# Row sums of two norms from two wide matmuls with ones as weights, in a single-core decoder block

## The chip, the core and the metric

The kernel runs on one core of a Trainium2 chip. Its time is device microseconds from start to end of one execution; the median over the runs is what counts. All matrix products are exact to nearly float32: each float32 operand is split into a high part and a low part (both of type `F32R`, which TensorE takes in one pass), and a product is the sum high*high + high*low + low*high, accumulated in float32.

## The reference

One block of a hybrid decoder over 512 positions and 1024 channels:

```python
def rmsnorm(x, g):
    y = x * lax.rsqrt(jnp.mean(x * x, axis=-1, keepdims=True) + EPS)
    return y * g

h = rmsnorm(x, norm1_g)                # norm 1
proj = h @ w_in                        # short conv, attention q/k/v, gates
...                                    # sparse attention, gated short conv
x = x + mix @ w_o
h = rmsnorm(x, norm2_g)                # norm 2
gu = h @ w_ffn_in                      # 1024 -> 2 x 2816
g = causal_dwconv(gu[..., :D_FF], ffn_conv_w) + ffn_conv_b
x = x + (silu(g) * gu[..., D_FF:]) @ w_ffn_out
```

Both norms need, for each of the 512 tokens, the sum of 1024 squares, and from it the factor r = (sum/1024 + eps)^-0.5.

## The kernel before

Channels lie on the 128 partitions (8 tiles of 128 channels), tokens along the free dimension (512). The norm's factor depends on the token alone, so the kernel multiplies by the gains at once, runs its products on the unscaled x, and applies r to the results. For r it squares each tile (ScalarE), adds the eight tiles up elementwise (`sq_sum` in norm 1, `sq2` in norm 2, 128x512 each), and then has to add over the 128 partitions. That is the work of `row_scales`. Before the change it goes like this, for four groups of 128 tokens:

1. Four float32 matmuls (L417): a 128x128 block of the summed squares is the weights, two columns of ones move through, and the result has the tokens on the partitions, two equal columns for each group, in a PSUM bank `pr`.
2. VectorE (L420) scales these 128x4 sums and adds eps into `ms`.
3. GpSimd (L411) raises `ms` to the power -0.5: `r`, 128x4, tokens on partitions.
4. Four transposes on TensorE (L426) of `r`, broadcast along the free dimension, bring r to all partitions with the tokens along the free dimension; ScalarE (L428) copies that from PSUM into `rb`.

**Norm 1** stands in the first stage, the token projection. `tok_round` walks over eight weight chunks k = 0..7; for token tiles 0 and 1 it runs 350-wide products into the banks `pj_s` (tile 0) and `pj_t`/`pj_o` (tile 1), `tok_products` being one chunk of one tile: products with the high weights at L219 and L220, with the low ones (`tok_lo`) at L222. At k = 6, `between` finishes an extra product `pkc` (compressed keys and values), has ScalarE copy it out of PSUM (`kv_evac`, `kc`, L471), and calls `row_scales`. VectorE and ScalarE then scale `pj_*` by r as they read the banks (`qkv`, L608 and L610). **Norm 2** stands between the output projection, whose loop ends with x in `x1` and its high and low forms `xf_h`, `xf_l`, and the feed-forward stage.

**The feed-forward stage** goes over 22 tiles of 128 inner channels, in pairs f = 0, 2, 4, ... For each pair there is a gate half (n = 0) and an up half (n = 1), and each half is a 2x2 block product made by seven products instead of eight (`ff_pair`; a11, a12, a22 and sums of them, named 1, 2, 3 and 4, are the forms of the weights, banks `p1`, `p26`, `p37`, `p45` take the results). Weights come in as two 512 KB loads for each half on SyncE's queue (`wr_s0_4` is half 0 of pair 4: in the order's names `wr_s0_40` and `wr_s0_41` are its two loads), through three buffers `wr` that the down-projection's loads `wr_d` share. A load is issued when the last reader of an older buffer is done.

The forms are made on ScalarE (`wh_s`, `sh`, `th`: high parts) and VectorE (`s32`, `s41`: sums of blocks at L945 to L950, `sl`, `tl`: low parts at L902). For some loads the low part is not made on VectorE: ScalarE writes the negated high part (`lo_by_dma`, L924, into `wl_s` or `wl_d`) and GpSimd starts a second, adding load of the same weights onto it (L927). The results are combined on VectorE (`c` for the gate, `up` for the up half, L1092 and L1120), multiplied by `rb_n2` (L1128, L1132), convolved (`cv`, L1074 to L1076) and passed through silu (L1077, ahead of whose first use ScalarE loads a function table), split (`ah`, `al`) and used by the down-projection (`pdn`).

The order of instructions on each engine is not written out by hand: the program is traced in a source order and a scheduler (`schedule_with_timeline_sim=True`, L1259) chooses each engine's order by a timeline of its own. `behind(later, earlier)` adds an order between two instructions. So an edit in one place can move instructions far from it.

Of the kernel before, what the change touches and what calls it, by code (L numbers as in the profile page):

```python
# [11 lines left out]
F32 = mybir.dt.float32  # L12
# [6 lines left out]
P = 128  # L19
D = 1024  # L20
# [71 lines left out]
def tile_block(ctx: ExitStack, tc: tile.TileContext, xT, pos, par, par2, w_tok, w_a3, w_gate, w_ao, w_bo, w_o,  # L92
# [93 lines left out]
        return hi, lo  # L186


    ones = const([P, P], "ones")
    nc.gpsimd.memset(ones, 1.0)  # L190
    warm = const([P, 1], "warm")
    wu = d_bank("wu")
# [19 lines left out]

    tok_lo = [y_tile(f"tok_lo{i}") for i in range(4)]

    def tok_products(tt, bank, k, wh, wl, first, last):
        ts_ = slice(tt * P, (tt + 1) * P)
        for c, (a, b) in enumerate(CH):
            acc = bank[c][:, :b - a]
            nc.tensor.matmul(acc, xg_h[:, k, ts_], wh[c], start=first, stop=False)  # L219
            nc.tensor.matmul(acc, xg_l[:, k, ts_], wh[c], start=False, stop=False)  # L220
        for c, (a, b) in enumerate(CH):
            nc.tensor.matmul(bank[c][:, :b - a], xg_h[:, k, ts_], wl[:, a:b], start=False, stop=last)  # L222
# [20 lines left out]
    def tok_round(tts, on_k, between):  # L243

        banks = [tok_banks(tt) for tt in tts]
        for k in range(KD):
            h = th.tile([P, TOKC], F32R, name=f"th{k}", tag="th", bufs=LAG) if k < LAG else None
            wh, wl = on_k(k, lambda first=0, then=None: load_w(w_tok[k], TOKC, f"t{tts[0]}{k}", first=first, mid=k > 0,
                                                               lo=tok_lo_of(k), hi=h, then=then, pieces=k == 0,
                                                               cuts=[b for _, b in CH] if k < 2 else ()))  # L250
            if k < LAG:
                kept.append(h)
            if k == KD - 2:
                between(k)
            if k < 2:
                first_products(tts, banks, k, [wh[:, a:b] for a, b in CH], wl)
            for tt, bank in zip(tts, banks) if k > 1 else ():
                tok_products(tt, bank, k, [wh[:, a:b] for a, b in CH], wl, k == 0, k == KD - 1)
            if k < KD - 2:
                between(k)  # L260
        return banks
# [148 lines left out]

        nc.gpsimd.tensor_tensor(dst, src, mhalf[:, :n], op=ALU.pow)  # L411

    def row_scales(total, name, bank_of):

        pr = bank_of(f"pr_{name}")
        for t in range(NT):
            sums = nc.tensor.matmul(pr[:, 2 * t:2 * t + 2], total[:, t * P:(t + 1) * P], ones[:, 0:2],  # L417
                                    start=True, stop=True)
        ms = sb.tile([P, NT], F32, name=f"ms_{name}", tag="ms")
        nc.vector.tensor_scalar(ms, pr[:, 0:2 * NT].rearrange("p (t two) -> p t two", two=2)[:, :, 0], 1.0 / D, EPS,  # L420
                                op0=ALU.mult, op1=ALU.add)
        r = sb.tile([P, NT], F32, name=f"r_{name}", tag=f"r_{name}")
        rsqrt(r, ms, NT)

        for t in range(NT):
            rows = nc.tensor.transpose(pr[:, t * P:(t + 1) * P], r[:, t:t + 1].to_broadcast([P, P]), ident)  # L426
        rb = sb.tile([P, S], F32, name=f"rb_{name}", tag="rb")
        nc.scalar.activation(rb, pr, AF.Copy)  # L428
        return r, rb, (sums, rows)

# [22 lines left out]
    def between(k):  # L455
        if k in kv_made:
            kv_made.pop(k)()
        if k == KD - 2:
            for kv in range(2):
                kc2.append(kv_evac(kv))  # L460
            scales1.extend(row_scales(sq_sum, "n1", d_bank))

    kv_made = {}
    kc2, scales1 = [], []
# [21 lines left out]
    for m, f in ((cm_add, NEG), (cm_one, 0.0)):  # L486
        nc.gpsimd.affine_select(out=m, in_=m, compare_op=ALU.is_ge, fill=f, base=-(CMPB - 1),
                                pattern=[[P, NT], [-STRIDE, NC]], channel_multiplier=1)
    r1, r1b, _ = scales1
    r1sq = const([P, S], "r1sq", F32, pb)  # L490
    nc.scalar.activation(r1sq, r1b, AF.Square)

# [560 lines left out]
        if n > 0:  # L1053
            nc.vector.tensor_add(sq2, sq2, sq)
    first_rest(0)
    _, r2b, (sums2, rows2) = row_scales(sq2, "n2", d_bank)
    mx_ctx.close()
    xv_ctx.close()

# [204 lines left out]
```

## Time and profile before

| | |
|---|---|
| Time, median of 3 runs | 724.91 us (724.86 to 725.02) |
| Profiled execution, its own time | 724.8 us |
| Its span on the core | 722.8 us (2.0 us lie around it) |
| TensorE (PE) busy | 717.5 us, 99% |
| Weight loads (PEld) busy | 638.6 us |
| VectorE (DVE) busy | 574.2 us, 79% |
| ScalarE (ACT) busy | 413.6 us, 57% |
| GpSimd (POOL) busy | 121.8 us, 17% |
| Granted TensorE clock | 1.00 throughout |

How to read it: rows of the timeline give start, duration, engine, line, operation, output<-inputs and the count of like instructions in the row, and in brackets the idle time of the engine ahead of it with what ended it. Matmuls are pipelined, so the duration of one is longer than its share of the engine: that share is the distance between two starts. An engine's share of busy time is a mean over stages with different limits.

### The profile page before, as it was taken

What the parts mean: (1) busy time and instruction counts of PE and PEld (TensorE: products, weight loads), DVE (VectorE), ACT (ScalarE), POOL (GpSimd) and SP (SyncE); (2) the same over time, 40 slices, a digit from 0 to 9 for tenths busy, and PEclk for the clock granted to TensorE, in tenths of its full rate; (3) what the DMA queues carried; (4) which work ended last, traced back from release to release, by engine and by line L of the source; (5) the groups of instructions that cost most, each with busy time, mean ns of one, the idle gap of its engine ahead of it and who ended that gap; (6) DMA issues with size and microseconds to landing.
All of it is one profiled execution on the core that took longest, in us unless ns stands there. A gap on an engine that the chain in (4) does not pass through costs nothing.

```text
span 722.8 us, 11204 instructions
## 1 busy us (share of the span) xinstructions
PE 717.5 (99%) x4281; PEld 638.6 (88%) x4281; DVE 574.2 (79%) x985; ACT 413.6 (57%) x705; POOL 121.8 (17%) x111
## 2 busy tenths in 40 slices
PE   9999999999999999999999999999999999999997
PEld 8999888888888888878889999999999999999986
DVE  7869967687666676787876999999898988979833
ACT  7666555777767676544665666565455554454320
POOL 1021443342343201232002011010000010000000
PEclk9999999999999999999999999999999999999999
DMA  8523552121111221336546466645655546552413
GB/s 311 209 74 110 156 129 64 65 78 58 59 59 59 72 75 59 100 134 203 175 131 161 109 154 167 183 119 133 163 141 129 134 129 156 125 146 88 117 30 117
DMA packets 36805, 88.21 MB, mean 122 GB/s; under 512 B 7440, under 2 KB 10896, under 8 KB 36752
## 3 DMA queue, kind: packets, MB, share of 16 engines
q1 hardware_dynamic: 30672, 74.42, 32.3%
q0 software_dynamic: 5648, 12.58, 10.6%
q8 instruction: 34, 0.56, 0.3%
q10 hardware_dynamic: 432, 0.49, 0.2%
q14 instruction: 19, 0.16, 0.1%
HBM read 85.39 MB, written 2.10 MB: 121 GB/s over the span
## 4 chain that ended last, share of the span: by engine, by line
PE 99%; DVE 0%; POOL 0%; issue 0%; POOLq 0%
PE p L147 10%; PE p L143 10%; PE p L140 10%; PE pdn L140 4%; PE pdn L143 4%; PE pg L145 4%; PE pg L140 4%; PE pg L143 4%; PE pdn L147 4%; PE pa L140 3%; PE pa L143 3%; PE pt L764 2%; PE po L140 2%; PE po L143 2%; PE po L147 2%; PE pa L147 2%
## 5 line engine op out<-in xcount | busy, mean ns | idle before, releaser
L140 PE MATMUL p<-xf_h,sh 128*128 128x256 f32 x352 | 87.4, 281 | 0.0
L143 PE MATMUL p<-xf_l,sh 128*128 128x256 f32 x352 | 87.2, 281 | 0.0
L140 PEld LDWEIGHTS p<-xf_h,sh 128*128 128x128 f32 x352 | 66.3, 188 | 0.0
L143 PEld LDWEIGHTS p<-xf_l,sh 128*128 128x128 f32 x352 | 66.3, 188 | 0.0
L901 ACT ACTIVATE sh<-s 128x1024 fp32r<-128x1024 f32 x44 | 45.6, 1050 | 19.1 <-DVE s L946 14.9
L902 DVE TENSOR_TENSOR sl<-s,sh 128x1024 fp32r<-128x1024 f32 x44 | 53.2, 1215 | 3.8 <-ACT sh L901 3.7
L147 PE MATMUL p<-xf_h,sl 128*128 128x256 f32 x352 | 55.8, 281 | 0.0
L927 POOL DMA_DIRECT2D wl_d<-in_w_dn_dram x16 | 19.1, 1195 | 208.3 <-ACT wl_d L924 208.3
L143 PE MATMUL pdn<-al,wh_d 128*128 128x512 f32 x134 | 52.6, 393 | 0.0
L140 PE MATMUL pdn<-ah,wh_d 128*128 128x512 f32 x134 | 52.2, 392 | 0.0
L140 PE MATMUL pg<-xg_h,wh_g 128*128 128x512 f32 x128 | 51.0, 399 | 0.0
L145 PE MATMUL pg<-xg_h,wl_g 128*128 128x512 f32 x128 | 50.8, 397 | 0.0
L143 PE MATMUL pg<-xg_l,wh_g 128*128 128x512 f32 x128 | 50.5, 395 | 0.0
L147 PEld LDWEIGHTS p<-xf_h,sl 128*128 128x128 f32 x352 | 47.9, 188 | 0.3
L715 ACT ACTIVATE e<-sc,mx 128x512 f32<-128x512 f32 (+3 forms) x64 | 33.2, 524 | 18.9 <-DVE mx L714 16.5
L140 PE MATMUL p<-xf_h,wh_s 128*128 128x256 f32 x176 | 43.5, 280 | 0.0
L143 PE MATMUL p<-xf_l,wh_s 128*128 128x256 f32 x176 | 43.4, 281 | 0.0
L140 PE MATMUL pa<-xg_h,wh_a 128*128 128x512 f32 x96 | 38.2, 398 | 0.0
L143 PE MATMUL pa<-xg_l,wh_a 128*128 128x512 f32 x96 | 37.9, 394 | 0.0
L768 DVE TENSOR_TENSOR pl<-pt,ph 128x512 fp32r<-128x512 f32 x40 | 27.3, 685 | 10.7 <-ACT ph L767 10.4
L741 ACT ACTIVATE e<-e,sums 128x512 f32<-128x512 f32 (+3 forms) x64 | 30.7, 554 | 7.5 <-DVE sums L691 7.5
L147 PE MATMUL pdn<-ah,wl_d 128*128 128x512 f32 x128 | 34.7, 393 | 0.0
(354 smaller groups left out, 2107.9 us busy)
## 6 DMA issues: line engine op xcount, KB each, us to landing
wr_s<-in_w_ff_dram SPq DMA_DIRECT2D x44, 512.0 KB, 3.9
wr_d<-in_w_dn_dram SPq DMA_DIRECT2D x22, 512.0 KB, 3.7
wr_g<-in_w_gate_dram SPq DMA_DIRECT2D x16, 512.0 KB, 3.5
wl_d<-in_w_dn_dram POOLq DMA_DIRECT2D x16, 512.0 KB, 7.4
wr_a<-in_w_a_dram SPq DMA_DIRECT2D x12, 512.0 KB, 3.4
wr_t<-in_w_tok_dram SPq DMA_DIRECT2D x10, 524.0 KB, 5.4
wr_o<-in_w_o_dram SPq DMA_DIRECT2D x8, 512.0 KB, 4.1
wr_ao<-in_w_ao_dram SPq DMA_DIRECT2D x4, 512.0 KB, 3.4
```

The source lines that it names most:

```text
L140: m = nc.tensor.matmul(acc, wh, xh, start=first and i == 0, stop=False)
L143: nc.tensor.matmul(acc, wh, xl, start=False, stop=False)
L145: m = nc.tensor.matmul(acc, wl, xh, start=False, stop=last and i == n - 1)
L147: m = nc.tensor.matmul(acc, wl, xh, start=False, stop=last and i == n - 1)
L715: nc.scalar.activation(e[:, i, 0:nk], sc[:, o:o + nk], AF.Exp, bias=mx[:, i], accum_out=sums[:, i])
L741: nc.scalar.activation(v, v, AF.Copy, scale=sums[:, i])
L764: ends["pt"] = nc.tensor.transpose(pt[:, i * P:(i + 1) * P], e[:, i, kt * P:(kt + 1) * P], ident)
L768: m = nc.vector.tensor_sub(pl, pt, ph.bitcast(F32))
L901: m = nc.scalar.activation(h, v, AF.Copy)
L902: nc.vector.tensor_sub(l, v, h.bitcast(F32))
L927: nc.gpsimd.dma_start(view(l), src, accum_op=ALU.add)
```

## The change

`row_scales` no longer takes the summed squares as weights. The squares are split into a high part (ScalarE copy to `F32R`) and a low part (VectorE subtraction), as the products' operands are (`in_parts`). Two matmuls with a 128x128 block of ones as weights take these two parts as moving data, 512 columns each, and accumulate in the same bank: every partition then holds every token's sum. VectorE multiplies the bank in place by the identity (broadcast over the four groups), which leaves on partition p only the four tokens p, 128+p, ..., and reduces over each group of 128 columns to `ms`, 128x4, which it scales as before. GpSimd's power is unchanged. The transposes and the copy to `rb` become a function `as_rows`, called later: in norm 1 after `tok_round` has been written, in norm 2 at once. For norm 1 the two parts take a buffer `sq_hl` of the tag `w4`, for norm 2 two buffers `sq2_h`, `sq2_l` of the tag `tb`. The last chunk's products (k = 7) in `tok_products` are put behind the sums.

```diff
--- before.py
+++ after.py
@@ -186,7 +186,8 @@
         return hi, lo
 
 
-    ones = const([P, P], "ones")
+    ones_r = const([P, P], "ones", F32R)
+    ones = ones_r.bitcast(F32)
     nc.gpsimd.memset(ones, 1.0)
     warm = const([P, 1], "warm")
     wu = d_bank("wu")
@@ -212,11 +213,13 @@
 
     tok_lo = [y_tile(f"tok_lo{i}") for i in range(4)]
 
-    def tok_products(tt, bank, k, wh, wl, first, last):
+    def tok_products(tt, bank, k, wh, wl, first, last, after=None):
         ts_ = slice(tt * P, (tt + 1) * P)
         for c, (a, b) in enumerate(CH):
             acc = bank[c][:, :b - a]
-            nc.tensor.matmul(acc, xg_h[:, k, ts_], wh[c], start=first, stop=False)
+            m = nc.tensor.matmul(acc, xg_h[:, k, ts_], wh[c], start=first, stop=False)
+            if after is not None:
+                behind(m, after)
             nc.tensor.matmul(acc, xg_l[:, k, ts_], wh[c], start=False, stop=False)
         for c, (a, b) in enumerate(CH):
             nc.tensor.matmul(bank[c][:, :b - a], xg_h[:, k, ts_], wl[:, a:b], start=False, stop=last)
@@ -255,7 +258,8 @@
             if k < 2:
                 first_products(tts, banks, k, [wh[:, a:b] for a, b in CH], wl)
             for tt, bank in zip(tts, banks) if k > 1 else ():
-                tok_products(tt, bank, k, [wh[:, a:b] for a, b in CH], wl, k == 0, k == KD - 1)
+                tok_products(tt, bank, k, [wh[:, a:b] for a, b in CH], wl, k == 0, k == KD - 1,
+                             scales1[-1] if k == KD - 1 else None)
             if k < KD - 2:
                 between(k)
         return banks
@@ -410,23 +414,34 @@
 
         nc.gpsimd.tensor_tensor(dst, src, mhalf[:, :n], op=ALU.pow)
 
-    def row_scales(total, name, bank_of):
+    def in_parts(total, h, l):
+        nc.scalar.activation(h, total, AF.Copy)
+        nc.vector.tensor_sub(l, total, h.bitcast(F32))
+        return h, l
+
+    def row_scales(name, bank_of, parts):
 
         pr = bank_of(f"pr_{name}")
-        for t in range(NT):
-            sums = nc.tensor.matmul(pr[:, 2 * t:2 * t + 2], total[:, t * P:(t + 1) * P], ones[:, 0:2],
-                                    start=True, stop=True)
+        h, l = parts
+        nc.tensor.matmul(pr, ones_r, h, start=True, stop=False)
+        sums = nc.tensor.matmul(pr, ones_r, l, start=False, stop=True)
+
+        pr4 = pr.rearrange("p (t c) -> p t c", c=P)
+        nc.vector.tensor_tensor(pr4, pr4, ident[:, None, :].to_broadcast([P, NT, P]), op=ALU.mult)
         ms = sb.tile([P, NT], F32, name=f"ms_{name}", tag="ms")
-        nc.vector.tensor_scalar(ms, pr[:, 0:2 * NT].rearrange("p (t two) -> p t two", two=2)[:, :, 0], 1.0 / D, EPS,
-                                op0=ALU.mult, op1=ALU.add)
+        nc.vector.reduce_sum(ms, pr4, axis=AX.X)
+        nc.vector.tensor_scalar(ms, ms, 1.0 / D, EPS, op0=ALU.mult, op1=ALU.add)
         r = sb.tile([P, NT], F32, name=f"r_{name}", tag=f"r_{name}")
         rsqrt(r, ms, NT)
 
-        for t in range(NT):
-            rows = nc.tensor.transpose(pr[:, t * P:(t + 1) * P], r[:, t:t + 1].to_broadcast([P, P]), ident)
-        rb = sb.tile([P, S], F32, name=f"rb_{name}", tag="rb")
-        nc.scalar.activation(rb, pr, AF.Copy)
-        return r, rb, (sums, rows)
+        def as_rows():
+
+            for t in range(NT):
+                rows = nc.tensor.transpose(pr[:, t * P:(t + 1) * P], r[:, t:t + 1].to_broadcast([P, P]), ident)
+            rb = sb.tile([P, S], F32, name=f"rb_{name}", tag="rb")
+            nc.scalar.activation(rb, pr, AF.Copy)
+            return rb, rows
+        return r, as_rows, sums
 
 
 
@@ -456,9 +471,11 @@
         if k in kv_made:
             kv_made.pop(k)()
         if k == KD - 2:
+            t = pp.tile([P, TOKC], F32R, name="sq_hl", tag="w4", bufs=NW4)
+            parts = in_parts(sq_sum, t[:, 0:S], t[:, S:2 * S])
             for kv in range(2):
                 kc2.append(kv_evac(kv))
-            scales1.extend(row_scales(sq_sum, "n1", d_bank))
+            scales1.extend(row_scales("n1", d_bank, parts))
 
     kv_made = {}
     kc2, scales1 = [], []
@@ -486,7 +503,8 @@
     for m, f in ((cm_add, NEG), (cm_one, 0.0)):
         nc.gpsimd.affine_select(out=m, in_=m, compare_op=ALU.is_ge, fill=f, base=-(CMPB - 1),
                                 pattern=[[P, NT], [-STRIDE, NC]], channel_multiplier=1)
-    r1, r1b, _ = scales1
+    r1, r1_rows, _ = scales1
+    r1b, _ = r1_rows()
     r1sq = const([P, S], "r1sq", F32, pb)
     nc.scalar.activation(r1sq, r1b, AF.Square)
 
@@ -1053,7 +1071,9 @@
         if n > 0:
             nc.vector.tensor_add(sq2, sq2, sq)
     first_rest(0)
-    _, r2b, (sums2, rows2) = row_scales(sq2, "n2", d_bank)
+    _, r2_rows, sums2 = row_scales("n2", d_bank, in_parts(sq2, *(pc.tile([P, S], F32R, name=f"sq2_{x}", tag="tb", bufs=3)
+                                                                 for x in "hl")))
+    r2b, rows2 = r2_rows()
     mx_ctx.close()
     xv_ctx.close()
```

The order of instructions changes in many places. Three of them matter below; the trailing numbers in names tell buffers apart.

First place: TensorE in norm 1, `pr_n1` being the bank of the sums. Before:

```order
L222 MATMUL pj_t10_103<-tok_lo3_93,xg_h_83 128x350
L222 MATMUL pj_t11_104<-tok_lo3_93,xg_h_83 128x350
L222 MATMUL pj_o1_105<-tok_lo3_93,xg_h_83 128x348
L219 MATMUL pj_s00_100<-wh_t07_465,xg_h_83 128x350
...
L219 MATMUL pj_t11_104<-wh_t07_465,xg_h_83 128x350
L417 MATMUL pr_n1_431<-ones_70,sq_sum_85 128x2 x4
L220 MATMUL pj_t11_104<-wh_t07_465,xg_l_84 128x350
...
L222 MATMUL pj_o1_105<-tok_lo3_93,xg_h_83 128x348
L426 MATMUL pr_n1_431<-ident_89,r_n1_438 128x128 x4
```

After:

```order
L225 MATMUL pj_t10_103<-tok_lo3_93,xg_h_83 128x350
L225 MATMUL pj_t11_104<-tok_lo3_93,xg_h_83 128x350
L225 MATMUL pj_o1_105<-tok_lo3_93,xg_h_83 128x348
L426 MATMUL pr_n1_434<-sq_hl_421,ones_70 128x512
L427 MATMUL pr_n1_434<-sq_hl_421,ones_70 128x512
L220 MATMUL pj_s00_100<-wh_t07_462,xg_h_83 128x350
...
L225 MATMUL pj_o1_105<-tok_lo3_93,xg_h_83 128x348
L440 MATMUL pr_n1_434<-ident_89,r_n1_441 128x128 x4
```

The sums moved ahead of all 18 products of chunk 7; before, 12 of these stood ahead of the sums and 6 behind them. The transposes stand behind the 18 in both.

Second place: TensorE and ScalarE around norm 2, where the feed-forward stage's first products have begun (`p11_0` and `p261_0` are banks of its up half, `p260_0` and `p370_0` of its gate half). Before, TensorE and then ScalarE:

```order
L140 MATMUL p11_0_4008<-xf_h_3502,wh_s1_0_3997 128x256
L417 MATMUL pr_n2_3867<-ones_70,sq2_3507 128x2 x4
L143 MATMUL p11_0_4008<-xf_l_3503,wh_s1_0_3997 128x256
...
L426 MATMUL pr_n2_3867<-ident_89,r_n2_3874 128x128 x4
L140 MATMUL p370_0_3891<-xf_h_3502,sh30_0_3319 128x256
```

```order
L901 ACTIVATE xf_h_3502<-xv3_3800 128x512 [waits DVE_49]
L924 ACTIVATE wl_s0_2_4112<-wr_s0_20_4107 128x1024 [waits DMAHW5_49,DVE_49]
L914 ACTIVATE wh_s0_2_4111<-wr_s0_20_4107 128x1024 [waits PE_49]
L958 ACTIVATE th1_0_4003<-wr_s1_01b_4001 128x512 [waits DMAHW4_49,PE_49]
```

After:

```order
L426 MATMUL pr_n2_3874<-sq2_h_3870,ones_70 128x512
L143 MATMUL p11_0_4015<-xf_l_3506,wh_s1_0_4004 128x256
...
L143 MATMUL p261_0_4016<-xf_l_3506,wh_s1_0_4004 128x256
L427 MATMUL pr_n2_3874<-sq2_l_3871,ones_70 128x512
L140 MATMUL p260_0_3897<-xf_h_3505,sh30_0_3322 128x256
...
L440 MATMUL pr_n2_3874<-ident_89,r_n2_3881 128x128 x4
L140 MATMUL p370_0_3898<-xf_h_3505,sh30_0_3322 128x256
```

```order
L418 ACTIVATE sq2_h_3870<-sq2_3510 128x512 [waits DVE_49]
L919 ACTIVATE xf_h_3505<-xv3_3803 128x512 [waits DVE_49]
L932 ACTIVATE wh_s0_2_4118<-wr_s0_20_4114 128x1024 [waits DMAHW5_49,PE_49]
L1118 ACTIVATE p11_0_4019<-p11_0_4015 128x256 [waits PE_49]
L942 ACTIVATE wl_s0_2_4119<-wr_s0_20_4114 128x1024 [waits DVE_49,PE_49]
```

The two sums stand ten products apart, and 63 products lie between the second and the transposes, where 39 lay before. On ScalarE the copy `wl_s0_2` stands behind `wh_s0_2` and a bank's evacuation, and now waits for TensorE: its buffer takes the memory of the squares' parts, which the second sum (L427) reads.

Third place: ScalarE in the stage's second and third pair. Before:

```order
L901 ACTIVATE sh31_2_4252<-s321_2_4249 128x1024 [waits DVE_49]
L1077 ACT_TABLE_LOAD
L1077 ACTIVATE cv0_3984<-cv0_3984 128x512 [waits DVE_49] x2
L901 ACTIVATE sh41_2_4259<-s411_2_4256 128x1024 [waits DVE_49]
L924 ACTIVATE wl_s0_4_4371<-wr_s0_40_4366 128x1024 [waits DMAHW1_49]
L914 ACTIVATE wh_s0_4_4370<-wr_s0_40_4366 128x1024 [waits PE_49]
```

After:

```order
L942 ACTIVATE wl_s0_4_4378<-wr_s0_40_4373 128x1024 [waits DMAHW1_49]
L932 ACTIVATE wh_s0_4_4377<-wr_s0_40_4373 128x1024
L919 ACTIVATE th0_2_4137<-wr_s0_21_4116 128x512 [waits DMAHW6_49,PE_49]
L1118 ACTIVATE p11_2_4278<-p11_2_4274 128x256 [waits PE_49]
L1097 ACT_TABLE_LOAD
L1097 ACTIVATE cv0_3991<-cv0_3991 128x512 [waits DVE_49] x2
```

The table load and the silu of pair 0 stood ahead of the copies that wait for pair 4's first load; they stand behind them now. On TensorE the first down-projection products (`pdn0_0` and `pdn1_0` with `wh_d00`) moved from behind pair 4's products on `sh40_4` to ahead of them. And on SyncE's queue the loads' buffers swapped: `wr_s0_40` now takes the buffer last read by the sum `s411_2` (L967 of the changed kernel); before it was the one last read by `tl0_2` (L902).

## The prediction

> **What bounds the kernel now.** I read the page first, then the waits of TensorE, then the stretches by stage, and last the timeline around the two norms and the first feed-forward pairs.
>
> ```profile
> PE 717.5 (99%) x4281; PEld 638.6 (88%) x4281; DVE 574.2 (79%) x985; ACT 413.6 (57%) x705; POOL 121.8 (17%) x111
> PE 99%; DVE 0%; POOL 0%; issue 0%; POOLq 0%
> PE wu L194 <- POOL ones L190: 1.1, 1, 1.1
> PE pr_n L426 <- POOL r_n L411: 0.3, 1, 0.3
> 36.00:45.00 9.00, 8.61 (x57) 8.12 (x56) 3.26 (x7) 7.30 (x17) 1.05 (x1) 1.00 0.43 117
> 400.00:460.00 60.00, 60.00 (x461) 57.83 (x461) 57.44 (x79) 35.55 (x45) 6.57 (x6) 1.00 0.60 150
> ```
>
> The chain that ended last is TensorE's own (PE, 99%). TensorE waits twice in the whole run: at the start, and 0.3 us in norm 1 for r. The stretch 36 to 45 (columns: length, then busy PE, PEld, DVE, ACT, POOL, clock, DMA share, GB/s) holds that gap; in 400 to 460, the first feed-forward pairs, TensorE has none, but VectorE is busy 57.44 of 60 us. So a matmul saved is time saved, and anything that makes a weight form late after 385 is a wait that the profile does not have yet.
>
> **The change part by part: norm 1.**
>
> ```profile
> 36.87 0.32 PE L219 MATMUL pj_s<-wh_t,xg_h 128*128 128x350 f32 x1
> ...
> 38.79 0.95 PE L417 MATMUL pr_n<-ones,sq_sum 128*128 128x2 f32 x8
> 39.59 0.41 PE L220 MATMUL pj_t<-wh_t,xg_l 128*128 128x350 f32 x1
> 39.84 0.32 PE L219 MATMUL pj_o<-wh_t,xg_h 128*128 128x348 f32 x1
> ...
> 41.12 0.65 PE L426 MATMUL pr_n<-ident,r_n 128*128 128x128 f32 x4 [0.33 <-POOL r_n L411]
> 28.43 0.39 PE L140 MATMUL pkc<-xg_h,wl_kv 128*128 128x512 f32 x1
> ...
> 28.89 0.39 PE L145 MATMUL pkc<-xg_h,wl_kv 128*128 128x512 f32 x1
> 39.77 0.16 DVE L420 TENSOR_SCALAR ms_n<-pr_n 128x4 f32<-128x4 f32 x1 [4.74 <-PE pr_n L417]
> 40.02 1.05 POOL L411 TENSOR_TENSOR r_n<-ms_n,mhalf 128x4 f32<-128x4 f32 x1 [15.45 <-DVE ms_n L420]
> 34.54 3.13 ACT L471 ACTIVATE kc<-pkc 64x256 f32<-64x256 f32 x8 [0.25 <-PE pkc L145]
> ```
>
> The four old sums hold TensorE from 38.79 to 39.59, 0.80 us, and the product behind them starts its successor after 0.25 instead of the usual 0.16 (36.87 to 38.79 is twelve products), 0.09 more. Two 512-wide matmuls take 28.43 to 28.89, 0.46. Saved: 0.43.
>
> The gap: between the sums and the transposes (41.12) TensorE ran out of products. Now the sums stand twelve products earlier. They need the bank that ScalarE's fourth copy of `pkc` frees, half of 3.13 after 34.54, thus 36.1, and TensorE gets there at 36.87: no wait, 0.8 in hand. They end at 36.87 + 0.46, with 0.16 of pipeline (0.39 less 0.23), 37.5. Then follow the multiply, the reduction, the scaling and the power:
>
> ```profile
> 386.12 0.69 DVE L1092 TENSOR_TENSOR c<-p,p 128x512 f32<-128x512 f32 x1 [0.45 <-PE p L147]
> L624 DVE TENSOR_REDUCE qst<-t x4: 941/944/977, 47.1 to 80.8; 128x12 f32<-128x768 f32 x4
> 28.15 1.08 ACT L171 ACTIVATE wh_t<-wr_t 128x1048 fp32r<-128x1048 f32 x1 [1.28 <-PE pj_o L220]
> 29.26 1.25 DVE L181 TENSOR_TENSOR tok_lo<-wr_t,wh_t 128x1048 fp32r<-128x1048 f32 x1 [0.88 <-ACT wh_t L171]
> ```
>
> Multiply 0.69 as the 128x512 that reads PSUM; no row shows a PSUM-to-PSUM one, so 0.6 to 1.2 (a second port to share at worst). Reduction two thirds of 0.94, 0.65. Scaling 0.16, power 1.05 (norm 2's took 1.47), with the 0.03, 0.09 and 0.05 that the old chain shows between engines and 0.06 between dependent VectorE steps: r at 40.35. TensorE reaches the transposes at 36.87 + 0.46 + 18 products of 0.16 = 40.2. So the transposes start at 40.35 instead of 41.12: 0.77 saved in norm 1, sums included. Bounds: 0.9 with no wait left; 0.3 with the power at 1.47 or the multiply at 1.2. The two new split instructions, some 0.6 each, fall into idle 1.28 us of ScalarE (ahead of 28.15) and 0.88 of VectorE (ahead of 29.26): nothing. Their cover gone, they would delay `tok_lo`, which TensorE reads at the end of a chunk.
>
> **Norm 2.**
>
> ```profile
> 383.25 0.95 PE L417 MATMUL pr_n<-ones,sq 128*128 128x2 f32 x8
> 384.06 0.49 PE L143 MATMUL p<-xf_l,wh_s 128*128 128x256 f32 x2
> ...
> 386.63 0.28 PE L140 MATMUL p<-xf_h,wh_s 128*128 128x256 f32 x1
> ...
> 387.34 0.64 PE L147 MATMUL p<-xf_h,wl_s 128*128 128x256 f32 x4
> 385.11 1.47 POOL L411 TENSOR_TENSOR r_n<-ms_n,mhalf 128x4 f32<-128x4 f32 x1 [0.22 <-DVE ms_n L420]
> ```
>
> The same sums, 0.81 and 0.09, give way to 0.46: 0.43 saved. A 256-wide product costs 0.118 (six from 386.63 to 387.34). The second sum comes 17 products behind 383.13, ends at 385.75, and 63 products lie ahead of the transposes, which TensorE reaches at 393.0. The power is now behind a load's start on GpSimd's queue; r is there by 391. No wait. The steps so far give 0.77 + 0.43 = 1.2 saved.
>
> **What moves in the feed-forward stage.** All times below are in the old run's clock; norm 1's gain shifts all engines alike.
>
> ```profile
> 384.58 1.06 ACT L914 ACTIVATE wh_s<-wr_s 128x1024 fp32r<-128x1024 f32 x1 [0.85 <-PE p L143]
> 385.74 20.13 SPq L907 DMA_DIRECT2D wr_s<-in_w_ff_dram  x4
> ...
> 403.61 2.25 SPq L907 DMA_DIRECT2D wr_s<-in_w_ff_dram  x2
> ...
> 391.35 1.06 ACT L924 ACTIVATE wl_s<-wr_s 128x1024 fp32r<-128x1024 f32 x1 [2.96 <-DMA wr_s<-in_w_ff_dram]
> 403.17 1.28 ACT L1077 ACT_TABLE_LOAD   x1
> 404.46 1.16 ACT L1077 ACTIVATE cv<-cv 128x512 f32<-128x512 f32 x2
> 408.46 1.06 ACT L924 ACTIVATE wl_s<-wr_s 128x1024 fp32r<-128x1024 f32 x1 [1.86 <-DMA wr_s<-in_w_ff_dram]
> 412.48 0.38 SPq L1150 DMA_DIRECT2D wr_d<-in_w_dn_dram  x1
> 418.40 1.04 ACT L1154 ACTIVATE wh_d<-wr_d 128x1024 fp32r<-128x1024 f32 x1
> 424.98 0.39 PE L140 MATMUL pdn<-ah,wh_d 128*128 128x512 f32 x1
> 422.50 1.05 ACT L924 ACTIVATE wl_s<-wr_s 128x1024 fp32r<-128x1024 f32 x1
> 423.84 0.91 POOL L927 DMA_DIRECT2D wl_s<-in_w_ff_dram  x1 [3.84 <-ACT wl_s L924]
> 431.70 0.64 PE L147 MATMUL p<-xf_h,wl_s 128*128 128x256 f32 x4
> DMA to landing us min/median/max: 5.5/5.6/7.0
> wr_ao<-in_w_ao_dram SPq DMA_DIRECT2D x4, 512.0 KB, 3.4
> ```
>
> The two lines at the end give issue to landing: of the four adding loads of `wl_s` (least, middle, most), and of a load with little beside it. I walk along the new order:
> 1. `wl_s0_2` stands behind `wh_s0_2` (ends 385.64), an evacuation (0.39) and the second sum: 386.0 to 387.1. SyncE's next load waits for it: 387.15 instead of 385.74, 1.4 late. Landing after 5.6 (385.74 to 391.35): 392.75.
> 2. Three ScalarE copies at 0.97 each: `sh30_2` at 395.75. VectorE then has nine steps without a pause up to `s411_2` (three of 128x1024 at 1.13, five of 128x512 at 0.60, one at 0.33): 402.05. `wr_s0_40` is issued there, 1.6 earlier than before (its buffer swapped).
> 3. Landing in 3.4 (quiet, `wr_ao`) to 4.85 (403.61 to 408.46 before): 405.5 to 406.9. Only behind that copy, `wh_s0_4`, `th0_2` and an evacuation does ScalarE load its table and make silu, which it had ready at 405.6: 5.3 later, 410.8 to 412.2. VectorE, whose next step needs silu, stands still meanwhile.
> 4. Nine VectorE steps, 5.6, after silu: 416.4 to 417.8. `wr_d00` waits for the last of them, `tl1_2`: 4 to 5.3 later than its 412.48. It lands after 3.5 to 4.9, two copies make `wh_d00` 422.0 to 424.7 (419.4 before). TensorE now wants it at 423.4: 255 products of 0.118 behind the transposes; it was 424.98.
> 5. Behind it on ScalarE: two convolution steps (1.4), `sh40_4` (1.05), `th0_4` (0.52), the copy for `wl_s1_4` (0.97): 426.0 to 428.7, against 423.55 before. GpSimd's adding load starts 0.3 later and lands after 5.6 to 7.0 (this load took 7.0, the most: 423.84 to 430.8, 0.9 ahead of the product at 431.70). So 431.9 to 436.0, and TensorE wants it at 431.0 (eight 512-wide products at 0.233 and 49 more behind 423.4).
>
> TensorE waits there 0.9 to 5.0; I take 2.4: landing near the quiet row in step 3 and 4, since no other load is in flight then, and 7.0 in step 5, where the same loads run beside it as before. Waits in steps 4 and 5 are not added, since the later contains the earlier. Places further on are late by the same amount, for all engines, and have that slack or more.
>
> A rule speaks against the change here. The Trainium skill ("ScalarE: Activation LUTs", What ACT_TABLE_LOAD costs) has about 1.38 us of drain behind a table load of 1.28. The rows agree with the load, but silu starts at 404.46, 0.01 behind it. By the rule the wait would be 1.4 longer; by the rows it is not, and I go by the rows.
>
> **Sum.** Against the profiled 724.8 (span 722.8 and 2.0 around it; median 724.91, 0.1 more): 724.8 - 1.2 + 2.4 = 726.0. That is 0.15% over the median; 0.2%, 1.45 us, is about what a measurement of this kernel can tell, so within 723.46 to 726.36 is "same".
>
> **Rivals.**
> - No wait in the feed-forward stage (the chain breaks somewhere: a load lands sooner, or a step doesn't wait as I read it). Then 724.8 - 1.2 = 723.6, with the gap wholly closed 723.4. For it: no wait there today. Against: the 0.9 in hand at 431.70 with the copy at least 2.4 later. Chance 0.18, of which 0.1 below 723.46.
> - Slower: the adding load of `wl_s1_4` is late by more than I take, because the loads of steps 3 and 4 need their 4.85 and it needs its 7.0 again. It decides from a copy ending at 426.5, where I take 426.1 (a wait of 2.8 instead of 2.4). 724.8 - 1.2 + 4 = 727.6, at most 728.6. For it: the row with 7.0. The Trainium skill ("DMA: Bandwidth & Descriptors", Issuing engines are not separate DMA queues) says that loads of all queues interleave on the same engines, which the 5.5 to 7.0 of equal loads fits. Chance 0.37.
> - Norm 1's chain is late (power 1.47, slow PSUM multiply): 0.5 less saved, 726.5 with the rest as forecast. For it: norm 2's row of 1.47. Chance 0.05, slower by a little.
>
> The forecast case, a wait of 1 to 2.8, has 0.4. Faster 0.1, same 0.08 + 0.4 = 0.48, slower 0.37 + 0.05 = 0.42. The range reaches from 723.5 (no wait) to 728.3 (a wait of 4.7).
>
> **What would show it.** Sums of two 512-wide matmuls 0.46 long, ahead of chunk 7; at the transposes of norm 1 a wait under 0.2; the silu's table load near 408, not 403; VectorE idle some 5 us between 404 and 412; among TensorE's waits new rows for `wl_s` (GpSimd) or `wh_d` (ScalarE) of 1 to 4 us at 423 to 433. The forecast is wrong if these waits are missing, or if waits appear ahead of 415, which step 2 excludes.

## The result, and the profile after

| | before | after |
|---|---|---|
| Time, median | 724.96 us (724.65 to 725.77, 6 runs) | 730.14 us (728.93 to 732.4, 6 runs) |
| Profiled execution, its span | 724.8, 722.8 us | 731.9, 730.0 us |
| Ratio after to before | | 1.0074, 95% interval 1.0056 to 1.0093 |

The change makes the kernel slower by 5.2 us. The forecast was 726.0 with a range of 723.5 to 728.3; the time lies above the range. The profiled execution, 731.9, is one of the two longest of the six, so the losses read from its rows come to 7.2 us, where the medians show 5.2.

The page's row of busy times of the changed kernel:

```profile
PE 720.6 (99%) x4269; PEld 638.8 (88%) x4269; DVE 578.0 (79%) x991; ACT 415.7 (57%) x707; POOL 121.1 (17%) x111
```

TensorE is at 99% as before; the average does not show the loss. Its waits do (us in total, times, longest):

```profile
PE p L147 <- DMA wl_s<-in_w_ff_dram: 3.3, 2, 2.8
PE p L140 <- ACT wh_s L932: 0.3, 1, 0.3
```

And so do the same stretches as before, with the one that holds the loss added (length, busy PE, PEld, DVE, ACT, POOL, granted clock, DMA share, GB/s):

```profile
36.00:45.00 9.00, 8.86 (x55) 8.28 (x54) 4.78 (x9) 7.73 (x17) 1.05 (x1) 1.00 0.44 117
400.00:460.00 60.00, 56.44 (x411) 53.08 (x410) 56.05 (x78) 35.16 (x44) 5.38 (x5) 0.97 0.60 149
430.00:440.00 10.00, 7.19 (x49) 6.99 (x49) 10.00 (x14) 5.81 (x8) 0.91 (x1) 0.83 0.81 187
```

The wait for r in norm 1 is gone, and TensorE's idle time in 36 to 45 falls from 0.39 to 0.14. But 400 to 460, where TensorE had no gap, now has 3.56 us of them, and a mean clock of 0.97; in 430 to 440 it is 0.83.

**Norm 1 and norm 2** in the timeline: the sums and transposes on TensorE, and norm 1's chain on VectorE and GpSimd (start, duration, engine, line):

```profile
37.17 0.40 PE L426 MATMUL pr_n<-sq_hl,ones 128*128 128x512 f32 x1
37.41 0.39 PE L427 MATMUL pr_n<-sq_hl,ones 128*128 128x512 f32 x1
37.64 0.32 PE L220 MATMUL pj_s<-wh_t,xg_h 128*128 128x350 f32 x1
...
40.75 0.65 PE L440 MATMUL pr_n<-ident,r_n 128*128 128x128 f32 x4
392.99 0.60 PE L440 MATMUL pr_n<-ident,r_n 128*128 128x128 f32 x4
37.93 0.70 DVE L430 TENSOR_TENSOR pr_n<-pr_n,ident 128x512 f32<-128x512 f32 x1 [2.54 <-PE pr_n L427]
38.67 0.69 DVE L432 TENSOR_REDUCE ms_n<-pr_n 128x4 f32<-128x512 f32 x1
39.65 1.05 POOL L415 TENSOR_TENSOR r_n<-ms_n,mhalf 128x4 f32<-128x4 f32 x1 [13.19 <-DVE ms_n L433]
```

Two wide sums hold TensorE from 37.17 to 37.64. Multiply 0.70, reduction 0.69, r at 40.70, the transposes at 40.75 without a wait. TensorE reached the sums 0.3 later than before (37.17 for 36.87), so against its own start it is 0.67 ahead behind these transposes.

**The feed-forward stage** in the timeline: SyncE, GpSimd, VectorE, ScalarE and TensorE along the chain of the prediction:

```profile
386.98 24.31 SPq L925 DMA_DIRECT2D wr_s<-in_w_ff_dram  x4
387.25 0.86 POOL L945 DMA_DIRECT2D wl_s<-in_w_ff_dram  x1 [1.34 <-ACT wl_s L942]
388.72 0.86 POOL L975 DMA_DIRECT2D tl<-in_w_ff_dram  x1 [0.61 <-ACT tl L974]
396.77 0.71 PE L147 MATMUL p<-xf_h,wl_s 128*128 128x256 f32 x4 [0.47 <-DMA wl_s<-in_w_ff_dram]
398.19 0.69 DVE L963 TENSOR_TENSOR s<-wr_s,wr_s 128x512 f32<-128x512 f32 x1 [3.03 <-DMA wr_s<-in_w_ff_dram]
404.41 1.22 DVE L1148 TENSOR_TENSOR c<-c,rb_n 128x1024 f32<-128x1024 f32 x1
405.72 1.53 ACT L1094 ACTIVATE cv<-c,par 128x512 f32<-128x512 f32 x2 [1.18 <-DVE c L1148]
407.15 1.05 ACT L942 ACTIVATE wl_s<-wr_s 128x1024 fp32r<-128x1024 f32 x1
409.95 1.28 ACT L1097 ACT_TABLE_LOAD   x1
411.25 1.16 ACT L1097 ACTIVATE cv<-cv 128x512 f32<-128x512 f32 x2
418.55 0.38 SPq L1170 DMA_DIRECT2D wr_d<-in_w_dn_dram  x1
427.19 1.05 ACT L942 ACTIVATE wl_s<-wr_s 128x1024 fp32r<-128x1024 f32 x1
428.54 0.91 POOL L945 DMA_DIRECT2D wl_s<-in_w_ff_dram  x1 [3.57 <-ACT wl_s L942]
436.21 1.22 PE L147 MATMUL p<-xf_h,wl_s 128*128 128x256 f32 x4 [2.81 <-DMA wl_s<-in_w_ff_dram]
437.23 0.41 PE L143 MATMUL p<-xf_l,wh_s 128*128 128x256 f32 x1
437.44 0.41 PE L140 MATMUL p<-xf_h,wh_s 128*128 128x256 f32 x1
```

The microsecond behind the wait as a stretch of its own (columns as above):

```profile
437.00:438.00 1.00, 1.00 (x7) 1.00 (x6) 1.00 (x2) 0.54 (x2) 0.00 (x0) 0.50 0.75 279
```

From issue to landing, the adding loads of `wl_s` (median 5.6 before) and then the loads of `wr_s` (most 7.1 before):

```profile
DMA to landing us min/median/max: 5.5/8.1/9.4
DMA to landing us min/median/max: 3.2/3.9/9.7
```

The reader should see four things. Four loads, three of them for pair 2, start together at 387 to 388.7. VectorE stands 3.03 us at 398.19 for one of them, `wr_s1_21` (issued at 388.46, landed at 398.11), and pair 0's gate (L1148) stands behind that on its queue. Silu comes at 411.25 instead of 404.46, and everything that hangs on it is late: the copy for `wl_s1_4` at 427.19 instead of 422.50, so its adding load starts at 428.54 and TensorE waits 2.81. And behind that wait the products come at 0.21 (437.23, 437.44) instead of 0.118, since the granted clock is 0.50.

Counted over TensorE's starts from 383 to 470, each against the usual distance for its width, the profiled run loses about 0.7 at 396, 1.3 in three short stops at 424 to 429 (for `wh_d00`, `sh40_4` and `wh_s1_4`), 3.0 at 433, 1.5 at half clock and 0.5 at 449.

### The profile page after: what moved, and what is told of

Read it like the earlier page. It is cut to its first block, busy times and chain, and to the rows that moved or that the text cites. A ratio compares the mean times of both kernels' runs of the same rounds, so it can differ in the third digit from the quotient of the medians.

```text
span 730.0 us, 11186 instructions
## 1 busy us (share of the span) xinstructions
PE 720.6 (99%) x4269; PEld 638.8 (88%) x4269; DVE 578.0 (79%) x991; ACT 415.7 (57%) x707; POOL 121.1 (17%) x111
## 4 chain that ended last, share of the span: by engine, by line
PE 90%; issue 5%; DMA 2%; ACT 1%; POOL 1%; DVE 0%; SPq 0%; POOLq 0%; DVEq 0%
PE p L147 8%; PE p L140 8%; PE p L143 8%; PE pdn L143 4%; PE pdn L140 4%; PE pg L145 4%; PE pg L140 4%; PE pg L143 4%; PE pdn L147 4%; PE pa L140 3%; PE pa L143 3%; PE pt L782 2%; PE po L143 2%; PE po L140 2%; PE po L147 2%
## 5 line engine op out<-in xcount | busy, mean ns | idle before, releaser
L919 ACT ACTIVATE th<-wr_s 128x512 fp32r<-128x512 f32 x20 | 12.6, 632 | 40.1 <-issue 29.1
```

The source lines that it names most:

```text
L919: m = nc.scalar.activation(h, v, AF.Copy)
```

## The experiments

All were timed against the kernel before on the same chip (medians 725.0, 725.02, 725.02 and 725.06 in the four groups). Theory A: norm 2's half makes the copy for `wl_s0_2` late (it waits for the second sum, whose parts lie in memory that its buffer takes over), four loads start together, and the rest follows. Theory B: the new order of VectorE and ScalarE in the first pairs loses the time by itself. Theory C: the wide sums cost by themselves. "The planner" is the scheduler that sets the order.

| run | median us | ratio, 95% interval |
|---|---|---|
| e1 norm 1 alone | 724.87 | 0.9996 (0.9988 to 1.0005) |
| e2 norm 2 alone | 731.31 | 1.0090 (1.0077 to 1.0103) |
| e7 own memory for norm 2's parts | 728.9 | 1.0051 (1.0036 to 1.0067) |
| e8 filler products in the wait | 729.87 | 1.0061 (1.0048 to 1.0073) |
| e13 own memory, old orders | 726.35 | 1.0017 (1.0007 to 1.0026) |
| e14 old orders | 725.44 | 1.0007 (0.9999 to 1.0016) |
| e15 old sums, new orders | 732.67 | 1.0098 (1.0082 to 1.0113) |
| e6 `wl_s1_4` without an adding load | 728.55 | 1.0057 (1.0043 to 1.0071) |
| e16 old VectorE and ScalarE order | 726.86 | 1.0030 (1.0018 to 1.0041) |
| e17 old VectorE order | 726.8 | 1.0030 (1.0018 to 1.0043) |
| e3 one rule for VectorE added | 725.6 | 1.0010 (1.0001 to 1.0018) |
| e4 one ScalarE step moved | 727.92 | 1.0043 (1.0030 to 1.0055) |
| e11 e3 and e7 together | 725.44 | 1.0007 (0.9998 to 1.0015) |
| e19 before, the rule of e3 reversed | 727.43 | 1.0034 (1.0021 to 1.0048) |

### Which norm: e1 and e2

e1 is the changed kernel with the old sums in norm 2, e2 with the old sums in norm 1 (`row_scales_old` is the old function).

```diff
-    _, r2_rows, sums2 = row_scales("n2", d_bank, in_parts(sq2, ...))
-    r2b, rows2 = r2_rows()
+    _, r2b, (sums2, rows2) = row_scales_old(sq2, "n2", d_bank)      # e1
-            scales1.extend(row_scales("n1", d_bank, parts))
+            scales1.extend(row_scales_old(sq_sum, "n1", d_bank))    # e2
```

> Norm 1 with the wide sums, norm 2 with the four narrow ones; the feed-forward stage's order on every engine is then that of the kernel before. Theory A (the loss comes from norm 2's half, through late loads in the first feed-forward pairs): 724.2 to 724.9, that is norm 1's 0.7 us less what the adding load of a11 at 91 takes back; no TensorE wait behind 380. Rival C (the wide sums and the PSUM steps cost time themselves, in both norms): 726 to 728.

> Norm 2 with the wide sums, norm 1 with the narrow ones; the order around and behind norm 2 is that of the changed kernel. Theory A: 729.5 to 730.8, the whole loss, with the wait of 2 to 3 us for wl_s1_4 near 434 and a dip of the granted clock behind it in most runs. Rival C: 727 to 728, half of the loss.

TensorE's waits in e2 (the first row is the one in question):

```profile
PE p L147 <- DMA wl_s<-in_w_ff_dram: 4.0, 2, 2.4
```

The whole loss is norm 2's half (e2 is 0.5 over its expectation). Norm 1's half has the same two wide sums, multiply and reduction, and costs nothing: C falls. It gains nothing that the timing can tell either. In e1's profiled run TensorE stays 0.78 ahead of the profiled run before up to the end, and over all runs of e1 the core's span is 0.8 shorter (medians 722.3 and 723.1). But 1.9 to 2.9 us lie around that span, where 1.9 to 2.1 did before, and what fills them the record does not show.

### The late copy: e7

```diff
-    ... in_parts(sq2, *(pc.tile([P, S], F32R, name=f"sq2_{x}", tag="tb", bufs=3) for x in "hl")))
+    sq2_hl = pw.tile([P, 2, half], F32R, name="sq2_hl", tag="sf", bufs=NSF)
+    ... in_parts(sq2, sq2_hl[:, 0], sq2_hl[:, 1]))
```

> The changed kernel, but the two parts of norm 2's squares lie in a buffer of the sums' tag sf instead of the pool pc, so that the copy wl_s0_2 no longer waits for the second wide sum and starts near 383 instead of 386; order of TensorE, and of all engines behind 390, as in the changed kernel. Theory A (the copy's wait starts four loads together at 387 to 389; wr_s1_21 then lands 5 us late and holds VectorE up 3 us at 395 to 398): wl_s0_2 lands before 391, wr_s1_21 by 395, VectorE's wait at 398 goes to under 0.5, everything behind it is 2.5 to 3 us earlier, the wait for wl_s1_4 falls from 2.8 to under 0.5, no clock dip: 724.0 to 725.2. Rival B (the new order of VectorE and ScalarE alone is enough): 728 to 730, with a wait of 2 us or more near 434.

In the timeline of e7, GpSimd's loads for `wl_s0_2` and `wl_s1_4`:

```profile
384.19 0.86 POOL L945 DMA_DIRECT2D wl_s<-in_w_ff_dram  x1 [1.15 <-ACT wl_s L942]
...
425.91 0.91 POOL L945 DMA_DIRECT2D wl_s<-in_w_ff_dram  x1 [3.57 <-ACT wl_s L942]
```

The landings of its `wl_s` loads:

```profile
DMA to landing us min/median/max: 5.3/5.6/8.5
```

And TensorE's wait in it:

```profile
PE p L147 <- DMA wl_s<-in_w_ff_dram: 3.5, 1, 3.5
```

The first load is 3 us earlier (387.25 in the changed kernel), VectorE has no wait at 398, and everything up to 426 runs 2.6 earlier. Yet only 1.2 us come back: the load at 425.91 is still 2.1 later than before (423.84), and it lands after 8.5, beside the loads around it. This profiled run, 731.16, is the longest of e7's six (the two shortest are 726.58 and 727.47), so its wait of 3.5 is more than the median has. A explains a part and no more.

### The half clock: e8

24 products with zero weights fill the place where TensorE waits.

```diff
+            ...
+            for k in range(FILL):                                  # FILL = 24
+                m = nc.tensor.matmul(b1[:, lo], zeros, xs[k % 4][0], start=False, stop=False)
+                behind(m, ends["t4"])
```

> The changed kernel with 24 products more, 256 wide, of zero weights added into the bank p11_4 just ahead of the products that wait for wl_s1_4: TensorE works through the wait (24 times 0.118 is 2.8 us) and its result is unchanged. If the idle wait makes the granted clock fall to half for some 3 us behind it (0.83 in 430 to 440), the clock stays at 1.00 here and the time is 1 to 2 us under the changed kernel's, 728.3 to 729.2, with a smaller spread. If the dip has another cause: 730 to 731 and a dip at the same place.

The stretch of the wait in e8 (columns as above):

```profile
430.00:440.00 10.00, 9.13 (x77) 8.93 (x77) 8.83 (x13) 5.54 (x7) 1.20 (x1) 1.00 0.58 153
```

The clock stays at 1.00, but the time, 729.87, is 0.7 over the expectation and within the spread of the changed kernel's. The filler moved other steps too (a wait of 1.1 for `wh_s` appeared), so this tells that the wait makes the clock fall, not what the fall is worth. The mean clocks of the single runs bound that. In the changed kernel the run with a clock of 1.000 took 728.93, the four at 0.997 and 0.998 took 729.57 to 731.9, and the one at 0.995 took 732.4. In e7 it is 726.58 and 727.47, then 728.7 to 729.76, then 731.16. A longer wait makes a run longer and its clock lower, so this is no clean price; in e6 the run at 1.000 (728.46) is no faster than those at 0.997.

### The order: e14, e13 and e15

From the first pair on, the positions of all instructions of TensorE, VectorE and ScalarE are fixed by a table, taken from the kernel before for e14 (changed kernel) and e13 (with e7's memory), and from the changed kernel for e15 (kernel before).

```diff
+    for e, order in FF_ORDER.items():
+        mine = [...]                     # what the engine was given behind norm 2, in source order
+        for a, b in zip(order, order[1:]):
+            tc.add_manual_dep(mine[b], mine[a].name, ...NoSync..., reason="order")
```

> The changed kernel, with norm 2's parts where the change puts them, so that the copy for wl_s0_2 still waits for the second sum (GpSimd's load 3 us late, four loads together at 387 to 389); but from the first feed-forward pair on TensorE, VectorE and ScalarE queue their instructions in the order of the kernel before. Theory A alone: most of the loss stays, 727.5 to 730, with waits at 396 (wl_s0_2) and 430 to 437. Theory B alone: 724.5 to 726, since silu is again ahead of the copy for wl_s0_4. If both are needed: 725.5 to 727.

> Both norms by wide sums, norm 2's two parts in a buffer that the copy for wl_s0_2 does not reuse, and from the first feed-forward pair on TensorE, VectorE and ScalarE queue their instructions in the order of the kernel before. Of the change only the sums themselves are left. Theory A (the late copy and the loads that then start together) and theory B (the new order of VectorE and ScalarE) both expect the loss gone: 724.3 to 725.2, no wait of TensorE over 0.5 us behind the start, wl_s1_4's adding load issued near 424. If it is 727 or more, the wide sums cost by something that neither theory names.

> The kernel before with its old sums in both norms, so that the copy for wl_s0_2 is not late; but from the first feed-forward pair on TensorE, VectorE and ScalarE queue their instructions in the order of the changed kernel. Theory A alone: 724.7 to 725.5, as before. Theory B alone: 727.5 to 730, with silu's table load near 407 and a wait of TensorE for wl_s1_4 of 2 us or more at 430 to 437.

Among TensorE's waits in e14, the one ahead of norm 2's transposes:

```profile
PE pr_n L571 <- POOL r_n L546: 1.1, 1, 1.1
```

Among its waits in e15, the one in the feed-forward stage:

```profile
PE p L278 <- DMA wl_s<-in_w_ff_dram: 3.9, 2, 2.9
```

In the timeline of e15, GpSimd's load for `wl_s0_2`, VectorE's wait and silu's table load:

```profile
387.70 0.92 POOL L1058 DMA_DIRECT2D wl_s<-in_w_ff_dram  x1 [1.46 <-ACT wl_s L1055]
397.63 0.69 DVE L1076 TENSOR_TENSOR s<-wr_s,wr_s 128x512 f32<-128x512 f32 x1 [1.60 <-DMA wr_s<-in_w_ff_dram]
409.38 1.28 ACT L1210 ACT_TABLE_LOAD   x1
```

Together they show that the loss lies in the order. With the old sums in both norms and only the new order it is all there, and 2.5 us more (e15 is 2.7 over its expectation); with the wide sums and the old order it is gone. But they do not part A from B as they were meant to. e15 has the bunched loads as well: ScalarE's new order puts `wl_s0_2`'s copy behind `wh_s0_2` and an evacuation, and its load starts at 387.70 though no second sum is there to wait for. And e14 has little of the late copy: in the old order the second sum stands two products behind the first, and the load for `wl_s0_2` starts at 385.13 (384.02 before), not at 387 as expected. What parts them is e7, which takes the late copy away and keeps most of the loss, and e3 below, which keeps the late copy and loses little. e14 shows why the wide sums gain nothing in norm 2 under the old order: there the transposes stand 40 products earlier, and r, now made by three VectorE steps with others between them, is not there for 1.1 us. e13 missed its expectation by 1.2. Its profiled run has 1.4 us of short waits for `wl_s` that e14's has not: `wr_s1_20` lands at 394.05, 1.7 later than in e14, and the load for `wl_s1_4` starts 1.7 later too. Why that load of the bunch was the late one is open.

### Which step: e17, e16, e3 and e4

e17 fixes VectorE alone to the old order, e16 VectorE and ScalarE. e3 and e4 leave the planner free but for one rule each:

```diff
-        nc.vector.tensor_sub(s[:, 0], a11, a21)
+        m = nc.vector.tensor_sub(s[:, 0], a11, a21)
+        if (f, n) == (2, 1):
+            behind(m, ends["c0"])       # e3; c0: the product of pair 0's gate with r
-            l = lo_by_dma(f"s{n}_{f}", raw, w_ff[f, n])
+            l = lo_by_dma(..., after=ends["silu1"] if (f, n) == (4, 0) else None)    # e4
```

> The changed kernel, with VectorE alone in the order of the kernel before from the first feed-forward pair on; TensorE and ScalarE as the planner then has them (wl_s0_2's copy stays behind wh_s0_2 and the second sum). If VectorE's order is the cause (its three subtractions for pair 2's second half stand behind pair 0's gate instead of ahead of it, so a late load no longer holds the gate): 724.3 to 726. If ScalarE's copies are the cause (four loads together at 387 to 389, the copy for wl_s0_4 ahead of silu): 727.5 to 730.

> The changed kernel, with VectorE and ScalarE in the order of the kernel before from the first feed-forward pair on, and TensorE's order left to the planner, which then puts norm 2's transposes where the changed kernel has them, 34 products later than the kernel before. If TensorE's own order has no part in the loss: no wait for wl_s1_4 at 430 to 437, and against the run with all three old orders (725.44) the wait of 1.1 us for r ahead of norm 2's transposes goes too: 724.0 to 724.9, the best of all. If TensorE's new order is part of the loss: 726.5 or more.

> The changed kernel with one more rule for the planner: VectorE's first subtraction for s321_2, which waits 3.0 us for wr_s1_21 in the changed kernel, stands behind the product of pair 0's gate with r. Silu comes earlier by itself. If that one place is the cause: silu's table load near 404, wl_s1_4's load issued before 426, 724.5 to 726.5. If not: 728 or more.

> The changed kernel with one instruction moved: ScalarE's copy for wl_s0_4 behind silu instead of ahead of it; nothing else changes its place. By the prediction's step 3 (silu waits for the landing of wr_s0_40): 725.5 to 727.5. If silu is late because VectorE's gate is (held by wr_s1_21): 729 to 731, as without the move.

In the timeline of e3, the gate, the subtraction that had waited, silu's table load, ScalarE's copy for `wl_s0_4` and GpSimd's load for `wl_s1_4`:

```profile
397.81 1.22 DVE L1150 TENSOR_TENSOR c<-c,rb_n 128x1024 f32<-128x1024 f32 x1
398.95 0.69 DVE L963 TENSOR_TENSOR s<-wr_s,wr_s 128x512 f32<-128x512 f32 x1
405.11 1.28 ACT L1099 ACT_TABLE_LOAD   x1
407.72 1.05 ACT L942 ACTIVATE wl_s<-wr_s 128x1024 fp32r<-128x1024 f32 x1
424.14 0.91 POOL L945 DMA_DIRECT2D wl_s<-in_w_ff_dram  x1 [2.62 <-ACT wl_s L942]
```

TensorE's wait for `wl_s` in e3:

```profile
PE p L147 <- DMA wl_s<-in_w_ff_dram: 0.2, 1, 0.2
```

Silu in e4, and after it TensorE's wait in e4:

```profile
409.24 1.15 ACT L1097 ACTIVATE cv<-cv 128x512 f32<-128x512 f32 x2
```

```profile
PE p L147 <- DMA wl_s<-in_w_ff_dram: 2.1, 2, 1.2
```

One rule on VectorE's queue gives back 4.5 of the 5.2 us. In e3 the gate goes first, at 397.81 instead of 404.41. `wr_s1_21` is late as in the changed kernel (8.8 us, landed at 396.89), VectorE does the gate's steps while it is on its way, and the subtraction behind the gate finds its data without a wait. But the rule moves more than that subtraction. All four VectorE steps for pair 2's sums now stand behind the gate, and the planner, left free, also puts silu ahead of the copy for `wl_s0_4` again (table load at 405.11, copy at 407.72) and changes TensorE's order. So the 4.5 is the price of these places together. The single ScalarE step of e4, which moves nothing else on the three engines, gives back 2.2, between its two expectations: silu comes without the copy for `wl_s0_4` ahead of it, 2.0 earlier than in the changed kernel (409.24 for 411.25), over half of that because the gate happened to be earlier too (403.25). The two do not add, since both shorten the same chain. e17 and e16 (726.8) gain less than e3. e17 lies between its two expectations. e16 is 2 over the better of its two and fits the other, by which TensorE's new order is part of the loss: it differs from e14 in that order alone, by 1.4 us. There the copy for `wl_s0_2` waits for the second sum again (its load starts at 386.71), `wr_s1_20` is the load of the bunch that lands late, and a wait of 1.4 for `wl_s` remains.

### The last load, and the two parts apart: e6, e11, e19

e6 takes (4,1) out of the list of low parts made by an adding load; e11 is e3 and e7 together; e19 puts e3's rule the other way round into the kernel before (`behind(ends["c0"], m)`).

> The changed kernel, but wl_s1_4 is made by VectorE from wr_s1_40 (a subtraction of 128x1024, 1.13 us) and not by a copy of ScalarE and an adding load of GpSimd. If that load's landing of 7.6 us is what TensorE pays for: the wait of 2.8 us and the clock dip go, 725.5 to 727.5. If everything is late by the order of VectorE and ScalarE and the load only came last: the wait goes to another form of pair 4 (wh_d00, sh31_4, wl_s1_4 by VectorE), 728 to 730.

> The changed kernel with two edits: VectorE's first subtraction for s321_2 behind the product of pair 0's gate with r, and norm 2's two parts in a buffer that the copy for wl_s0_2 does not reuse. If the held gate was the cause and the late copy only what held it: 724.2 to 725.6, no wait of TensorE over 0.5 us behind the start, and none for wl_s0_2 at 396; the second edit is then worth 0.2 to 0.7 against 725.6. If both norms' shorter sums are worth what the prediction said (1.2), 723.7 to 724.2.

> The kernel before, old sums in both norms, with one more rule for the planner: VectorE's product of pair 0's gate with r stands behind the first subtraction for s321_2, as in the changed kernel. Here wr_s1_21 lands near 393.4, ahead of that subtraction. If the place on VectorE's queue costs only where that load is late: 724.7 to 726. If the place alone is enough (silu behind the copy for wl_s0_4): 727 or more, with a wait for wl_s1_4.

TensorE's wait in e6, and then the stretch that holds it:

```profile
PE p L140 <- ACT sh L919: 2.2, 1, 2.2
```

```profile
430.00:440.00 10.00, 7.80 (x50) 7.08 (x49) 10.00 (x14) 5.86 (x7) 0.76 (x1) 0.83 0.45 145
```

Without the load, TensorE gets a few products further and then waits for `sh` of pair 4, which the extra VectorE step of 1.13 makes later still. 1.6 us come back: the load came last, but pair 4's other forms are late as well. e11 (725.44) is within 0.2 of e3, so once the gate does not stand behind the late load, the late load costs next to nothing. e19 shows the other side, in the timeline of VectorE and ScalarE:

```profile
396.89 0.69 DVE L945 TENSOR_TENSOR s<-wr_s,wr_s 128x512 f32<-128x512 f32 x1
397.50 1.22 DVE L1130 TENSOR_TENSOR c<-c,rb_n 128x1024 f32<-128x1024 f32 x1
...
407.10 1.07 ACT L924 ACTIVATE wl_s<-wr_s 128x1024 fp32r<-128x1024 f32 x1 [0.67 <-DMA wr_s<-in_w_ff_dram]
...
409.02 0.62 ACT L1079 ACTIVATE cv<-cv 128x512 f32<-128x512 f32 x1
```

Here `wr_s1_21` is in time and the subtraction delays the gate by one step only. Still 2.4 us are lost: the planner then puts half of silu behind the copy for `wl_s0_4`, which waits for its load, and other ScalarE steps move as well. So this is not a test of that one place alone, and how the 2.4 divide is open.

No version beats the kernel before beyond what the timing can tell; e1, 724.87, is nearest.

## Why the prediction was wrong

**What held.** The sums take 0.47 (0.46 forecast), the multiply 0.70 and the reduction 0.69 (0.69 and 0.65), norm 1's transposes do not wait, norm 2's stand at 392.99 (393.0). The path of the loss is the one forecast: a late copy for `wl_s0_2`, silu behind the copy for `wl_s0_4`, `wr_d00` late, `wl_s1_4`'s load late. Silu is ready at 412.41 (410.8 to 412.2), the copy for `wl_s1_4` ends at 428.24 (426.0 to 428.7), and the wait is 2.81 (0.9 to 5.0, 2.4 taken). The drain behind a table load that the Trainium skill states ("ScalarE: Activation LUTs", What ACT_TABLE_LOAD costs), and that was weighed against the rows, does not show: silu starts 0.02 behind the load (409.95 + 1.28, 411.25).

**The step that failed** is the second of the chain: "VectorE then has nine steps without a pause". Step 1 let `wr_s1_20` land in 5.6 (it took 3.9) and asked nothing of `wr_s1_21`, whose load starts 1.5 behind it, with two adding loads of GpSimd beside them. `wr_s1_21` took 9.7 (5.8 before), and VectorE stood 3.03 us for it with pair 0's gate behind. The step's sum is off as well: its nine steps as counted come to 6.7, not to the 6.3 that lead to 402.05; in the trace they are two of 128x1024, six of 128x512 and one of 128x256, 6.2 without the wait. That step also excluded waits ahead of 415; one of 0.47 stands at 396.77. The 5 us that VectorE was to stand idle between 404 and 412 did not come: it stood 0.90, ahead of 412.44, since its work had been pushed back to there. And step 3 had silu wait for the landing of `wr_s0_40`; the rows show that copy (407.15) without a wait, and the convolution ahead of it waiting for the gate. That load had landed only 0.15 earlier (407.00), held up behind the same VectorE steps, so the time of silu came out nearly right by luck.

**The terms that were mis-sized.** The wait itself came out close, 2.81 for 2.4; most of the miss lies in terms that the sum put at nothing. The load of step 5 took 7.6, where 5.6 to 7.0 were allowed. With the forecast's 431.0 that would have been a wait of 5.2, but TensorE came 2.4 later. It had lost 2.0 of these at 396 and in the short stops at 424 to 429 for `wh_d00`, `sh` and `wh_s`, which the sum lacked ("waits in steps 4 and 5 are not added" left out that other forms of pair 4 are late as well). Both hang on the late copy and the step that failed: in e7's profiled run, without VectorE's wait, neither is there. Missing too is the half clock behind the wait, 1.5, and about 1.0 in small stops behind 445. VectorE's wait is not the whole of it, though: e7 has none, and its median of 728.9 still lies above the range.

**The gain of 1.2 did not arrive.** Norm 1's 0.67 is in the rows of the profiled run but no longer at 91, where an adding load of `wl_a` landed 8.6 us after its issue (6.9 before) and held TensorE; in e1 it stays up to the end of the core's span, and even there the medians of the time differ by 0.1 only. Norm 2's 0.43 is less than the wait of 1.1 for r where the transposes stand as before.

**The rivals.** "Slower" had the right mechanism, but its most was 728.6: it knew one late load and one wait. The rule of the Trainium skill cited for it ("DMA: Bandwidth & Descriptors", Issuing engines are not separate DMA queues) agrees with the trace: a load of SyncE that took 5.8 with the kernel before, where one load of GpSimd's started within 1.5 us of it, took 9.7 where two did. It bore on step 1 as much as on step 5, and there it was not applied.

## What to carry to other kernels

When a planner sets the order, compare the whole queues and ask of every transfer that moves what is queued behind the instruction that waits for it: here four subtractions ahead of another pair's gate, and with them silu behind a copy, cost 4.5 us, while each half of the edit that was priced was worth under 1. Price a load by what else starts within two microseconds of it, on any queue. And add up all that is late on a path, not its last wait only: a wait of TensorE past 2 us cost more than itself here, 1.5 us at half clock behind 2.81.

## What the hardware showed

In the profiled runs TensorE's granted clock fell to 0.50 with each longer wait and not with short ones. In the changed kernel it fell near the end of a wait of 2.81, at 435.8, and stayed at half for 3.4 us, 3.0 of them behind the wait. In e7 and e15, with waits of 3.5 and 2.9, it stayed there for 6.8. In e6, with one of 2.2, it fell only 1.5 us after TensorE was back at work (434.5 and 436.0). A gap of 1.4 left it alone. That is e16, its longest wait for `wl_s` and then its stretch:

```profile
PE p L177 <- DMA wl_s<-in_w_ff_dram: 1.9, 2, 1.4
```

```profile
430.00:440.00 10.00, 8.61 (x71) 8.32 (x70) 10.00 (x14) 5.75 (x7) 1.20 (x1) 1.00 0.56 159
```

The Trainium skill ("TensorE: Matmul & The Clock Gate", Why this matters for your kernels) warns of gaps over about 3 us. Here one of 2.2 was enough, and those of 1.4 and less were not.
